# Sums of squares of eight norms: two products of 12-bit parts with ones in the place of one fp32 product

## Chip, cores and metric

The kernel runs on one core of a Trainium2 chip. The metric is the device time of one execution in microseconds; for the kernel before it is the median of three timed runs. One further execution was profiled; its trace is what the rows below come from.

## What is computed

Two transformer blocks follow each other on one sequence of 256 tokens with 1024 channels, each block with two layers, all in fp32. The first block has, per layer, a feed-forward, a hybrid mixer (a recurrent branch, an attention branch and a convolution branch) and a second feed-forward; the second block has a mixer and a feed-forward with a short convolution. Each of these parts begins with a norm:

```python
def rms_norm(x, g):
    xf = x.astype(jnp.float32)
    y = xf * lax.rsqrt(jnp.mean(xf * xf, axis=-1, keepdims=True) + NORM_EPS)
    return (y * g.astype(jnp.float32)).astype(x.dtype)

for l in range(DEPTH):
    x = x + 0.5 * swiglu(rms_norm(x, ffn1_norm[l]), ffn1_w1[l], ffn1_w2[l])
    x = x + hybrid_mixer(rms_norm(x, mix_norm[l]), positions, w_in[l], ...)
    x = x + 0.5 * swiglu(rms_norm(x, ffn2_norm[l]), ffn2_w1[l], ffn2_w2[l])
```

The change concerns the mean of squares in it, which is one number for each token, summed over 1024 channels.

## The kernel before

Activations lie with channels on the partitions: x is a tile of 128 partitions x 8 groups x 256 tokens, so a sum over channels is one over 8 groups (elementwise adds) and one over 128 partitions. A weight slab of 1024 columns is loaded by a DMA that SyncE issues (raw), rounded to 12-bit mantissas by ScalarE (wh, line 206) and its remainder taken by VectorE (wl, line 206 too). Activations are split the same way (xh and xl; hh and hl for the hidden units, function split, lines 511 to 513). Each product of fp32 matrices is then three products of such parts (mm3, lines 235 to 237): wh with xh, wh with xl, wl with xh. A slab feeds 24 of them, each with 128 x 128 weights and 256 columns. Six buffers each of wh and wl let ScalarE and VectorE work ahead of TensorE; four of raw let the transfers work ahead of them.

The norm is spread out. While x is written, Next.take splits x times the gain at once, without the root, and class Stat collects the squares: ScalarE squares each group (line 481, tile sq), VectorE adds them up (line 489, tile sqa). Stat.done (line 494) sums over the partitions: a product of a 128 x 128 tile of ones with the last sqa, in fp32, gives every partition the whole sum in a PSUM tile o. ScalarE makes the factor R of it in two activations (rstd_from, lines 466 and 467: logarithm and exponential). The products of the first weights run meanwhile on the values without the factor, and VectorE applies R to their sums when it reads them out of PSUM (line 620 in the first block's feed-forwards, line 1298 in the second's; in the mixers line 541 makes normalised values of x). So the work around a norm does not stop for it: the sum of squares is called from inside the first loop over weights (function linears, argument between; first_pairs for feed-forwards).

Seven PSUM banks hold sums of the feed-forward products (four in mixers); a bank is free again when VectorE has read it.

What sets the order on each engine is a scheduler that places the instructions by its own estimates of when operands are there; within an engine the queue is then strictly in order. Dependencies added by hand (behind) and program order for table loads bind it in some places. Stat.done has two further forms: late (the norm behind a part of the second block, which adds a second fp32 product) and tok (the norm ahead of the second block's mixer, which also wants the sum with tokens on partitions).

At the start, ScalarE's queue issues the DMA of the first 128 rows of parameters (line 122), which TensorE transposes (line 129) ahead of x itself (line 378).

Of the kernel before, what the change touches and what calls it, by code (L numbers as in the profile page):

```python
# [8 lines left out]
F32R = mybir.dt.float32r  # L9
# [7 lines left out]
P = 128  # L17
T = 256
# [25 lines left out]
def f32(ap):  # L44
    return ap.bitcast(F32)
# [95 lines left out]
def kernel(ctx: ExitStack, tc: tile.TileContext, p, out: bass.AP):  # L141
    nc = tc.nc
    V, S, G, PE = nc.vector, nc.scalar, nc.gpsimd, nc.tensor

    const = ctx.enter_context(tc.tile_pool(name="const", bufs=1))
    wpools = [ctx.enter_context(tc.tile_pool(name="w", bufs=6))]
    act = ctx.enter_context(tc.tile_pool(name="act", bufs=1))
# [136 lines left out]
    def linps():  # L284
        return banks['lin'].tile([P, 512], F32, name="lin")
# [2 lines left out]
    ident = const.tile([P, P], F32, name="ident")  # L288
    ones = const.tile([P, P], F32, name="ones")
    G.memset(ones, 1.0)  # L290
    G.affine_select(out=ident, in_=ones, pattern=[[-1, P]], compare_op=ALU.is_equal, fill=0.0, base=0,
                    channel_multiplier=1)
    epsc = const.tile([P, 1], F32, name="epsc")
# [22 lines left out]
    start = ctx.enter_context(ExitStack())  # L316
# [58 lines left out]
    for k in range(KD):  # L375
        ps = linps()
# [85 lines left out]
    def rstd_from(dst, ps, n, eps=epsc):  # L462

        t = tmp.tile([P, T], F32, name="sq")
        w = dst.shape[-1]
        S.activation(t[:, :w], ps, AF.Ln, scale=1.0 / n, bias=eps)
        S.activation(dst, t[:, :w], AF.Exp, scale=-0.5)
# [5 lines left out]
    class Stat:  # L473
# [17 lines left out]

        def done(self, tok=False):
            ps = pso.tile([P, 512], F32, name="o")
            PE.matmul(ps[:, :T], ones, self.acc, start=True, stop=not self.late)
            if self.late:
                PE.matmul(ps[:, :T], ones, self.sq, start=False, stop=True)
            r = act.tile([P, T], F32, name="R", bufs=2)
            rstd_from(r, ps[:, :T], D)
            if not tok:
                return r  # L500
            ps = banks['att'].tile([P, 512], F32, name="pt")
            for t in range(2):
                PE.matmul(ps[:, t:t + 1], self.acc[:, t * P:(t + 1) * P], ones[:, 0:1], start=True, stop=True)
            rt = act.tile([P, 2], F32, name="Rt", bufs=2)
            rstd_from(rt, ps[:, 0:2], D)
            return r, rt

    def split(h, lo, src, scale=None):

        if scale is None:  # L510
            return S.copy(h, src), V.tensor_tensor(lo, src, f32(h), op=ALU.subtract)
        return (S.activation(h, src, AF.Copy if isinstance(scale, float) else AF.Identity, scale=scale),
                V.scalar_tensor_tensor(lo, src, scale, f32(h), op0=ALU.mult, op1=ALU.subtract))
# [920 lines left out]
```

## Time and profile before

| | us |
|---|---|
| median of three timed runs | 1889.68 |
| lowest and highest of them | 1886.5, 1891.59 |
| the profiled execution | 1880.21 |
| its span, from first to last instruction | 1878.5 |

| engine | busy, us | share of the span |
|---|---|---|
| TensorE, products | 1850.9 | 99% |
| TensorE, weight loads | 1809.4 | 96% |
| VectorE | 1491.8 | 79% |
| ScalarE | 1121.2 | 60% |
| GpSimd | 75.8 | 4% |

How to read it: a product's row shows the time from its start to the modelled end, 0.28 us for an ordinary one, while products start every 0.11 us; so the cost of a product on TensorE is read from the starts of its neighbours. An fp32 product appears as two records. A share that is an average over the span says little about single places: VectorE's 79% has stretches of 100%.

### The profile page before, as it was taken

What the parts mean: (1) busy time and instruction counts of PE and PEld (TensorE: products, weight loads), DVE (VectorE), ACT (ScalarE), POOL (GpSimd) and SP (SyncE); (2) the same over time, 40 slices, a digit from 0 to 9 for tenths busy, and PEclk for the clock granted to TensorE, in tenths of its full rate; (3) what the DMA queues carried; (4) which work ended last, traced back from release to release, by engine and by line L of the source; (5) the groups of instructions that cost most, each with busy time, mean ns of one, the idle gap of its engine ahead of it and who ended that gap; (6) DMA issues with size and microseconds to landing.
All of it is one profiled execution on the core that took longest, in us unless ns stands there. A gap on an engine that the chain in (4) does not pass through costs nothing.

```text
span 1878.5 us, 38913 instructions
## 1 busy us (share of the span) xinstructions
PE 1850.9 (99%) x15292; PEld 1809.4 (96%) x15292; DVE 1491.8 (79%) x3041; ACT 1121.2 (60%) x1895; POOL 75.8 (4%) x225
## 2 busy tenths in 40 slices
PE   8999999999999999999999999999999999999998
PEld 8999999999999999999999999989999998999997
DVE  7778799897766776799987766888799778779983
ACT  6545777575555555668566555466666545757663
POOL 8000000000000000000000000110000011000000
PEclk9999999999999999999999999999999999999999
DMA  8656545556656665653546666561366647135652
GB/s 260 205 176 197 176 142 158 183 168 202 193 189 200 192 195 182 189 179 127 169 157 214 191 193 190 152 213 46 113 210 199 207 127 235 53 123 173 209 199 82
DMA packets 329879, 327.36 MB, mean 174 GB/s; under 512 B 16956, under 2 KB 323648, under 8 KB 329696
## 3 DMA queue, kind: packets, MB, share of 16 engines
q1 hardware_dynamic: 326336, 322.71, 55.2%
q0 software_dynamic: 3344, 2.16, 0.5%
q8 instruction: 120, 1.97, 0.4%
q14 instruction: 63, 0.52, 0.1%
q10 hardware_dynamic: 16, 0.00, 0.0%
HBM read 323.76 MB, written 1.05 MB: 173 GB/s over the span
## 4 chain that ended last, share of the span: by engine, by line
PE 93%; ACT 2%; DVE 2%; DMA 2%; issue 1%; SPq 0%; DVEq 0%; ACTq 0%
PE lin L235 27%; PE lin L236 27%; PE lin L237 27%; PE o L673 2%; PE lin L278 2%; PE lin L280 1%; PE lin L279 1%; PE sc L668 1%; PE pt L659 1%; DMA raw<-in_w_in_dram 1%; ACT wh L206 1%; DVE wl L206 1%; PE sc L667 1%; PE o L674 1%; DMA raw<-in_ffn_w_dram 0%
## 5 line engine op out<-in xcount | busy, mean ns | idle before, releaser
L206 DVE TENSOR_TENSOR wl<-raw,wh 128x1024 fp32r<-128x1024 f32 (+2 forms) x644 | 748.5, 1168 | 267.9 <-ACT wh L206 267.1
L206 ACT CAST wh<-raw 128x1024 fp32r<-128x1024 f32 (+2 forms) x644 | 644.6, 1005 | 473.7 <-PE lin L236 321.1
L235 PE MATMUL lin<-xh,wh 128*128 128x256 f32 (+1 forms) x3120 | 866.1, 279 | 3.8 <-ACT wh L206 2.3
L236 PE MATMUL lin<-xl,wh 128*128 128x256 f32 (+1 forms) x3120 | 869.4, 279 | 0.0
L237 PE MATMUL lin<-xh,wl 128*128 128x256 f32 (+1 forms) x3120 | 868.2, 279 | 0.0
L235 PEld LDWEIGHTS lin<-xh,wh 128*128 128x128 f32 (+1 forms) x3120 | 584.6, 188 | 6.7 <-ACT wh L206 2.9
L236 PEld LDWEIGHTS lin<-xl,wh 128*128 128x128 f32 (+1 forms) x3120 | 588.0, 189 | 0.7
L237 PEld LDWEIGHTS lin<-xh,wl 128*128 128x128 f32 (+1 forms) x3120 | 586.1, 188 | 0.5
L235 PE MATMUL lin<-hh,wh 128*128 128x256 f32 x880 | 243.0, 276 | 0.0
L236 PE MATMUL lin<-hl,wh 128*128 128x256 f32 x880 | 242.9, 276 | 0.0
L237 PE MATMUL lin<-hh,wl 128*128 128x256 f32 x880 | 242.9, 276 | 0.0
L235 PEld LDWEIGHTS lin<-hh,wh 128*128 128x128 f32 x880 | 165.2, 188 | 0.0
L236 PEld LDWEIGHTS lin<-hl,wh 128*128 128x128 f32 x880 | 165.2, 188 | 0.0
L237 PEld LDWEIGHTS lin<-hh,wl 128*128 128x128 f32 x880 | 165.2, 188 | 0.0
L235 PE MATMUL lin<-r,wh 128*128 128x256 f32 x372 | 105.6, 284 | 0.8 <-ACT f L898 0.5
L237 PE MATMUL lin<-r,wl 128*128 128x256 f32 x372 | 104.9, 282 | 0.0
L932 DVE SCALAR_TENSOR_TENSOR f<-f,pcol,f 128x256 f32<-128x256 f32 x240 | 103.9, 482 | 0.9
L236 PE MATMUL lin<-r,wh 128*128 128x256 f32 x372 | 103.9, 279 | 0.0
L622 ACT ACTIVATE sg<-g 128x256 f32<-128x256 f32 x88 | 35.6, 413 | 61.1 <-DVE g L620 61.0
L235 PEld LDWEIGHTS lin<-r,wh 128*128 128x128 f32 x372 | 70.1, 188 | 1.9 <-ACT f L898 0.9
L236 PEld LDWEIGHTS lin<-r,wh 128*128 128x128 f32 x372 | 70.0, 188 | 0.4
L237 PEld LDWEIGHTS lin<-r,wl 128*128 128x128 f32 x372 | 69.9, 188 | 0.2
(435 smaller groups left out, 2348.7 us busy)
## 6 DMA issues: line engine op xcount, KB each, us to landing
raw<-in_ffn_w_dram SPq DMA_DIRECT2D x256, 512.0 KB, 3.7
raw<-in_w_in_dram SPq DMA_DIRECT2D x116, 512.0 KB, 3.6
raw<-in_w_up_dram SPq DMA_DIRECT2D x88, 512.0 KB, 3.7
raw<-in_w_down_dram SPq DMA_DIRECT2D x42, 512.0 KB, 3.4
raw<-in_w_out_dram SPq DMA_DIRECT2D x32, 512.0 KB, 3.7
raw<-in_w_in_dram SPq DMA_DIRECT2D x32, 256.0 KB, 3.5
raw<-in_ffn_w_dram SPq DMA_DIRECT2D x16, 256.0 KB, 3.1
raw<-in_lru_w_out_dram SPq DMA_DIRECT2D x8, 512.0 KB, 4.7
```

The costliest lines, as they stand in the source:

```text
L206: i = S.copy(dst(h), src(raw)), V.tensor_tensor(dst(lo), src(raw), f32(dst(h)), op=ALU.subtract)
L235: PE.matmul(ps, wh, xh, start=first, stop=False)
L236: PE.matmul(ps, wh, xl, start=False, stop=False)
L237: PE.matmul(ps, wl, xh, start=False, stop=last)
L278: PE.matmul(ps, xh, wh, start=first and k == 0, stop=False)
L279: PE.matmul(ps, xh, wl, start=False, stop=False)
L280: PE.matmul(ps, xl, wh, start=False, stop=last and k == kt - 1)
L622: S.activation(sg_, g, AF.Silu)
L659: PE.transpose(pt[:, i * P:(i + 1) * P], e[:, i * P:(i + 1) * P], ident)
L667: PE.matmul(sc[:, 0:P], q[:, 0:P], k[:, 0:P], start=True, stop=True)
L673: PE.matmul(o[:, 0:T], v[:, 0, :], pt[:, 0:T], start=first, stop=False)
L932: i = V.scalar_tensor_tensor(cc[:, c, :], pcin[:, c, j:j + T], prm('cdw', l, 4 * j + c), cc[:, c, :], op0=ALU.mult, op1=ALU.add)
```

## The change

A second tile of ones, onesr, of the type fp32r (the one of the split parts), is made once at the start by ScalarE; it is a stretch of a tile twice as wide, so that later tiles keep their place within a kilobyte. In Stat.done the forms late and tok stay as they were. In the plain form, which eight norms use (the two feed-forwards and the mixer of both layers of the first block, and the feed-forwards of the second block), sqa is split into sah (ScalarE) and sal (VectorE), and two products with onesr add up both parts in the same PSUM tile.

```diff
+    onesr = const.tile([P, 2 * P], F32R, name="onesr")[:, 48:48 + P]
+    S.copy(onesr, ones)
...
-            PE.matmul(ps[:, :T], ones, self.acc, start=True, stop=not self.late)
-            if self.late:
-                PE.matmul(ps[:, :T], ones, self.sq, start=False, stop=True)
+            if self.late or tok:
+                PE.matmul(ps[:, :T], ones, self.acc, start=True, stop=not self.late)
+                if self.late:
+                    PE.matmul(ps[:, :T], ones, self.sq, start=False, stop=True)
+            else:
+
+                ah, al = (act.tile([P, T], F32R, name="sa" + q) for q in "hl")
+                split(ah, al, self.acc)
+                PE.matmul(ps[:, :T], onesr, ah, start=True, stop=False)
+                PE.matmul(ps[:, :T], onesr, al, start=False, stop=True)
```

The new instructions also make the scheduler order others anew. Line numbers of the new kernel are higher by 3 from line 291 on and by 10 behind Stat.done.

ScalarE at the norm of the first feed-forward. Line 481 (484) squares, line 206 converts a weight slab, lines 466 and 467 (469 and 470) make R, line 622 (632) begins the feed-forward's activations. Before:

```order
L481 ACTIVATE sq<-x 128x256
L206 CAST wh<-raw 128x1024 x2
L466 ACTIVATE sq<-o,epsc 128x256
L467 ACTIVATE R<-sq 128x256
L206 CAST wh<-raw 128x1024
L622 ACT_TABLE_LOAD
```

The same place now:

```order
L484 ACTIVATE sq<-x 128x256
L206 CAST wh<-raw 128x1024
L521 CAST sah<-sqa 128x256
L206 CAST wh<-raw 128x1024
L469 ACTIVATE sq<-o,epsc 128x256
L206 CAST wh<-raw 128x1024
L470 ACTIVATE R<-sq 128x256
L206 CAST wh<-raw 128x1024
L632 ACT_TABLE_LOAD
```

The new copy stands behind one conversion of weights, and a further conversion has come between the two activations that make R.

TensorE at the norm of the first block's mixer in layer 0 (o is the PSUM tile of the sum of squares, lin one of the weight products). Before:

```order
L235 MATMUL lin<-xh,wh 128x256
L236 MATMUL lin<-xl,wh 128x256
L237 MATMUL lin<-xh,wl 128x256
L494 MATMUL o<-sqa,ones 128x256
L235 MATMUL lin<-xh,wh 128x256
```

The same place now:

```order
L237 MATMUL lin<-xh,wl 128x256
L505 MATMUL o<-sah,onesr 128x256
L235 MATMUL lin<-xh,wh 128x256
L236 MATMUL lin<-xl,wh 128x256
L506 MATMUL o<-sal,onesr 128x256
```

The first product stands where the old one stood, the second two products later. In the first feed-forward the first stands three products later than the old one and the second eight behind it; in the second block's feed-forwards four later and six behind; in the other three feed-forwards both stand at the old place.

VectorE at the norm of the second block's first feed-forward (line 1298, now 1308, reads the sums out of PSUM with R). Before:

```order
L489 TENSOR_TENSOR sqa<-sqa,sq 128x256
L206 TENSOR_TENSOR wl<-raw,wh 128x1024 x2
L1298 TENSOR_TENSOR up_17796<-lin,R 128x256
L1298 TENSOR_TENSOR up_17797<-lin,R 128x256
L1298 TENSOR_TENSOR up_17798<-lin,R 128x256
L1302 SCALAR_TENSOR_TENSOR u<-up_17796,pcol_1980,u 128x256
```

The same place now:

```order
L492 TENSOR_TENSOR sqa<-sqa,sq 128x256
L206 TENSOR_TENSOR wl<-raw,wh 128x1024
L521 TENSOR_TENSOR sal<-sqa,sah 128x256
L206 TENSOR_TENSOR wl<-raw,wh 128x1024 x2
L1308 TENSOR_TENSOR up_17828<-lin,R 128x256
L1308 TENSOR_TENSOR up_17829<-lin,R 128x256
```

The subtraction stands between two conversions of weights, and a third conversion has moved ahead of the first reading; the fourth one, too, stands earlier than before among the operations of line 1312 (1302). From there the order on VectorE and ScalarE differs for the next hundred microseconds.

## Rows read from the trace of the kernel before

**Rows 1.** The page: busy time (share) and count; the chain that ended last.

```profile
PE 1850.9 (99%) x15292; PEld 1809.4 (96%) x15292; DVE 1491.8 (79%) x3041; ACT 1121.2 (60%) x1895; POOL 75.8 (4%) x225
...
PE 93%; ACT 2%; DVE 2%; DMA 2%; issue 1%; SPq 0%; DVEq 0%; ACTq 0%
```

**Rows 2.** Timeline, TensorE, third site: start, length, operation, idle before.

```profile
426.63 0.28 PE L236 MATMUL lin<-xl,wh 128*128 128x256 f32 x1
...
427.20 0.59 PE L494 MATMUL o<-sqa,ones 128*128 128x256 f32 x2
...
427.75 0.28 PE L236 MATMUL lin<-xl,wh 128*128 128x256 f32 x1
```

**Rows 3.** Groups by line, 0 to 60 us: count, busy us, mean ns, idle.

```profile
L511 DVE TENSOR_TENSOR hl<-u,hh 128x256 fp32r<-128x256 f32 x8 | 3.0, 418 | 0.0
L511 ACT CAST hh<-u 128x256 fp32r<-128x256 f32 x8 | 2.9, 402 | 0.9 <-DVE u L625 0.9
```

**Rows 4.** Timeline, VectorE and ScalarE, ahead of the third site.

```profile
421.48 0.42 DVE L489 TENSOR_TENSOR sqa<-sqa,sq 128x256 f32<-128x256 f32 x1
...
421.84 1.05 ACT L206 CAST wh<-raw 128x1024 fp32r<-128x1024 f32 x1 [0.95 <-PE lin L236]
```

**Rows 5.** Timeline, VectorE, ScalarE and TensorE, first site.

```profile
24.69 0.42 DVE L489 TENSOR_TENSOR sqa<-sqa,sq 128x256 f32<-128x256 f32 x1
...
25.41 1.05 ACT L206 CAST wh<-raw 128x1024 fp32r<-128x1024 f32 x1 [1.59 <-DMA raw<-in_ffn_w_dram]
...
25.53 0.59 PE L494 MATMUL o<-sqa,ones 128*128 128x256 f32 x2
...
26.49 1.23 DVE L206 TENSOR_TENSOR wl<-raw,wh 128x1024 fp32r<-128x1024 f32 x1 [1.39 <-ACT wh L206]
```

**Rows 6.** Timeline, VectorE and TensorE, second site (mixer, layer 0).

```profile
197.37 0.42 DVE L489 TENSOR_TENSOR sqa<-sqa,sq 128x256 f32<-128x256 f32 x1
197.71 0.82 DVE L206 TENSOR_TENSOR wl<-raw,wh 128x640 fp32r<-128x640 f32 x1
...
197.77 0.28 PE L237 MATMUL lin<-xh,wl 128*128 128x256 f32 x1
197.88 0.66 PE L494 MATMUL o<-sqa,ones 128*128 128x256 f32 x2
...
198.50 0.28 PE L236 MATMUL lin<-xl,wh 128*128 128x256 f32 x1
```

**Rows 7.** Timeline, ScalarE, VectorE and TensorE, seventh site (second block, layer 0).

```profile
1350.36 1.04 ACT L206 CAST wh<-raw 128x1024 fp32r<-128x1024 f32 x1
...
1351.05 2.35 DVE L206 TENSOR_TENSOR wl<-raw,wh 128x1024 fp32r<-128x1024 f32 x2
1353.32 1.07 DVE L1298 TENSOR_TENSOR up<-lin,R 128x256 f32<-128x256 f32 x3
...
1362.30 1.22 DVE L206 TENSOR_TENSOR wl<-raw,wh 128x1024 fp32r<-128x1024 f32 x1
...
1351.43 0.59 PE L494 MATMUL o<-sqa,ones 128*128 128x256 f32 x2
```

**Rows 8.** Timeline, ScalarE and TensorE, the start.

```profile
1.85 1.28 ACT L471 ACT_TABLE_LOAD   x1 [1.85 <-POOL ident L291]
...
8.99 1.04 ACT L206 CAST wh<-raw 128x1024 fp32r<-128x1024 f32 x1 [1.35 <-DMA raw<-in_ffn_w_dram]
...
3.48 0.45 PE L129 MATMUL lin<-ident,prow 128*128 128x128 f32 x1 [3.48 <-POOL crow L336]
...
5.06 3.46 PE L378 MATMUL lin<-ident,xin 128*128 128x128 f32 x15 [0.91 <-DMA xin<-in_x_dram]
```

**Rows 9.** Windows: stretch, length, busy (count) by engine, granted clock, DMA share.

```profile
12.50:16.20 3.70, 3.70 (x21) 3.70 (x20) 3.70 (x8) 3.20 (x6) 3.13 (x7) 0.54 0.94 272
...
1360.00:1380.00 20.00, 20.00 (x179) 20.00 (x179) 19.94 (x39) 13.15 (x22) 0.00 (x0) 1.00 0.63 195
```

**Rows 10.** Timeline, TensorE, the first weight product.

```profile
10.09 0.38 PE L235 MATMUL lin<-xh,wh 128*128 128x256 f32 x1 [1.57 <-ACT wh L206]
```

## Prediction

> **What bounds the kernel now.** I read the page first. TensorE is busy in 99% of the span, and the chain that ended last runs 93% over it [rows 1]: what a stage is worth on the other engines counts only where TensorE then waits. So the question for each of the eight changed norms is a small one: how many steps does TensorE's queue spend on the sum of squares, and does it stand still for the operands? For that I read the timelines of TensorE, ScalarE and VectorE around each place. The eight, in order of time, are: first block, layer 0, feed-forward 1 (25.53 us) [rows 5], mixer (197.88) [rows 6], feed-forward 2 (427.20) [rows 2]; layer 1 the same three; then the feed-forward of the second block's two layers (the first at 1351.43) [rows 7]. I call them sites 1 to 8.
>
> **Part 1: the product itself.** At site 3 nothing waits. Five products lie between 426.63 and 427.20, so an ordinary step is 0.57/5 = 0.114 us. From the fp32 product's start at 427.20 to the second product behind it at 427.75 pass 0.55 us; with one ordinary step taken off, the fp32 product costs 0.44 us of TensorE's queue [rows 2]. Its place is taken by two products of the kind that the whole kernel consists of (fp32r weights, 256 fp32r columns): 2 x 0.114 = 0.23. Saved: 0.21 us a site, 1.7 us for eight, if neither new product waits.
>
> **Part 2: the split.** ScalarE gets a copy that rounds to 12 bits (sah), VectorE a subtraction (sal). The same pair exists for the hidden units: 0.40 us and 0.42 us [rows 3]. Both engines have idle time, so the 8 x 0.4 us are no cost in themselves. What costs is that sah must follow the last sum sqa, sal must follow sah, each in its engine's queue behind a weight conversion, and TensorE takes its queue in order.
>
> *Sites 3, 4 and 6.* sqa is ready 5 us before TensorE gets there (last sum 421.48 to 421.90, product at 427.20), and ScalarE idles 0.95 us ahead of its next conversion [rows 2, 4]. Both parts are ready long before. Full gain: 3 x -0.21 = -0.6.
>
> *Site 1.* Here sah stands behind a weight conversion that itself waited 1.59 us for its transfer and ran 25.41 to 26.46; sqa was ready at 25.11 [rows 5]. So sah ends at about 26.8, and with the 0.09 us that pass between an end and the waiting product (197.79 to 197.88) [rows 6] TensorE may start it at 26.9. In the new order it comes three products later than the old one, at 25.53 + 3 x 0.114 = 25.87: a stand of 1.0 us. Eight products on, at 26.9 + 9 x 0.114 = 27.9, comes sal, which VectorE can begin only after its own conversion (26.49 to 27.72) [rows 5], so it ends at 28.1: another 0.2. Net: 1.2 + 0.23 - 0.44 = +1.0 us. TensorE never gets that back, since it has no idle time behind it to eat.
>
> R then is later by more than 1 us, also because a third conversion now stands between the two activations that make it. TensorE needs the first accumulator back only at product 156 of the stage, 44 products (5 us) behind the norm, and comes there later by 1.2 us itself. I count nothing, with 0.5 us as the upper bound.
>
> *Sites 2 and 5.* The old product already started at the moment that sqa came: end at 197.79, product at 197.88 [rows 6]. Now sah runs 197.88 to 198.28 and TensorE starts at 198.37 instead of 197.88: 0.49. Two products later (198.71) it wants sal, which follows VectorE's 640-column conversion (to 198.53) and ends at 198.87, so 198.96: 0.25. New cost 0.49 + 0.25 + 0.23 = 0.97; the old one is 198.50 - 197.77 less two steps = 0.50. Site 5 has the same order on all three engines. Net 2 x 0.47 = +0.9.
>
> *Sites 7 and 8.* sqa is complete when VectorE's next conversion starts, 1351.05; sah follows ScalarE's conversion that ends at 1351.40, so it is there at 1351.8. The new order has moved the product four steps back, to 1351.43 + 0.45 = 1351.88: no wait. sal follows the conversion that starts at 1351.05 (two of them take 2.35 us, so one ends near 1352.2) and ends near 1352.6; it is wanted six products later, at 1352.67 [rows 7]. No wait, by a hair: 2 x -0.21 = -0.4.
>
> **Part 3: what R's delay does at sites 7 and 8.** sal moved back makes R about 1.0 us later, and a third conversion now stands ahead of VectorE's first read of the sums (1353.32 before). I get 1354.8. Behind it VectorE is full: 19.94 of 20 us between 1360 and 1380 [rows 7, 9]. What it owes TensorE is wl. In the old order the fourth wl behind the norm was written from 1362.30 to 1363.52, and its slab (24 products; 81 of the stage lie ahead of the norm) is entered at about 1364.5, its first wl product two steps later: 1.2 us of margin. The new order pulls the third and the fourth wl ahead by several operations, which gives this slab more, and leaves the delay to later slabs. So I take 0 here, with the whole delay of 1.5 us a site as the bound; that is the likeliest way to a real loss.
>
> **Part 4: the start.** onesr is made by ScalarE ahead of everything else in its queue, including the DMA that brings the first parameter rows; and this first copy carries a table load of its own. The row of a table load is 1.28 us, with the next instruction free to start at once [rows 8]. With it and a 0.4 us copy, the DMA of those parameters, whose place was just ahead of the old first table load at 1.85, goes out 1.3 to 1.7 us later, and the transposes of the parameters (3.48) with it; those of x ran mostly from 5.06, held by their own data. They shift by 0.1 to 0.6 us. The first products wait for the conversion at 8.99, and that waits for its transfer with 1.35 us of ScalarE idle ahead of it [rows 8], so the cover is thicker than the shift: I take +0.1.
>
> The Trainium skill, page "ScalarE: Activation LUTs", section "What ACT_TABLE_LOAD costs", says that a switch of set costs about 1.28 us of load and about 1.38 us of drain. The load agrees with the row; the drain does not show in it. By the page the DMA would be another 1.4 us late, the shift at most 2.0 us against 1.35 of cover, and the sum up to 0.7 us higher (an estimate from that page).
>
> **Sum.** +1.0 (site 1) + 0.9 (2, 5) - 0.6 (3, 4, 6) - 0.4 (7, 8) + 0.1 (start) = +1.0 us. Against the profiled execution (1880.2 us, span 1878.5) that is 1881.2. The three timed runs of before lie higher, at 1886.5 to 1891.6, median 1889.7; the change has nothing to do with that offset, so I forecast 1890.7 for the median after.
>
> **Rivals.**
> *The parts are always ready.* If the order is right about when sah and sal come, all eight sites gain: -1.7 us, 1888.0. For it speaks that five or six sites show room; against it the rows of sites 1, 2 and 5, where the operand was just in time or its engine stood waiting. It would need ScalarE's transfer at site 1 to come a microsecond sooner. Chance 0.15, and still within 0.3% (5.7 us, about what a measurement of this kernel can tell from no change).
> *The clock falls at site 1.* TensorE's granted clock was 0.54 between 12.50 and 16.20, mostly at 1.2 instead of 2.4 GHz, after it had waited 1.57 us at 10.09 and again shortly after [rows 9, 10]. That stretch held 21 products in 3.70 us, which at 0.114 take 2.4: 1.3 us lost. A stand of 1.0 + 0.2 is near enough that it can happen again: 1892.0. Chance 0.2; also within 0.3%.
> *Slower: VectorE runs out of wl at sites 7 and 8.* If the reordered half of these stages (both feed-forwards are ordered anew for some 100 us) leaves VectorE later than its margin, TensorE stands for the difference at each slab where it is, until the margin is back. It decides from 1.2 us of delay beyond what the moved conversions give back. With 3 us at each site: 1890.7 + 6 = 1897. For it: VectorE's 19.94 of 20 us; against it: two conversions are pulled forward, and no wait of the product of that stage shows before. Chance 0.1.
> *Not what it says:* if products with onesr cost as much as fp32 ones, each site pays 0.65 more: 5 us, 1896. Every other product with fp32r operands steps at 0.114, so 0.02.
> *Faster by over 0.3%:* nothing in the sum can give more than 1.7 us; only a side effect that I don't see (all later tiles lie 1 or 3 KB further on in each partition), or the runs' own spread: 0.05.
>
> **How the numbers follow.** The forecast's own case has 0.48; with the first two rivals 0.83 lies within 0.3%. Slower by over 0.3% takes the third and fourth rival: 0.12. The range: the low end is the first rival less half the spread of the runs (2.5 us): 1885.5; the high end reaches to the slower rival's time: 1896.5.
>
> **What would show it.** In the profile after, TensorE's list of waits has the sah product for about 1 us once and 0.5 us twice, and the sal product for 0.2 to 0.3 three times, nowhere else; the step of both is 0.114; the sites at 427, 607 and 1011 show no wait and lie 0.2 closer to their neighbours. Waits for wl inside the last two feed-forwards would prove the slower rival; a clock below 1 near 27 us the second. I would be wrong if TensorE stands at sites 7 or 8, or if ordinary steps change from 0.114.

## The result, and the profile after

The change made the kernel slower by 1%, where I had forecast +1.0 us.

| | before | after |
|---|---|---|
| median of six runs each, us | 1885.7 | 1901.56 |
| lowest, highest | 1873.45, 1891.59 | 1897.98, 1908.75 |
| ratio after to before | | 1.0099, interval 1.0071 to 1.0128 |
| profiled execution, span | 1878.5 | 1899.8 |

With the later series before was timed 117 times in all (medians of the series 1879 to 1886, lowest run 1873.1, highest 1906.4) and after 18 times (median 1901.1, 1878.0 to 1913.3). That single runs of one kernel lie 30 us apart is part of the finding. In the second series of after the ratio reads 1.0031, because comparisons leave out runs over 1.5% above the fastest, which here drops runs that are long for the reason told below; the medians give 1899.38/1886.13 = 1.0070.

The page of after, busy times with counts and the chain that ended last [rows 1 before]:

```profile
PE 1869.7 (98%) x15292; PEld 1826.1 (96%) x15292; DVE 1497.9 (79%) x3049; ACT 1125.3 (59%) x1905; POOL 75.5 (4%) x225
...
PE 84%; DVE 10%; ACT 2%; DMA 2%; issue 1%; SPq 0%; DVEq 0%; ACTq 0%
```

As many products as before (one fp32 product was two records, so is a pair), 18.8 us longer busy. TensorE hardly waits more: the rows of its list of waits add up to 23.4 us against 20.9. It is the products themselves. Windows with nothing but ordinary products, of before and then of after (stretch, length, busy (count), granted clock, DMA share, GB/s):

```profile
60.00:120.00 60.00, 60.00 (x532) 1.00 0.62 194
450.00:600.00 150.00, 150.00 (x1326) 1.00 0.61 193
1040.00:1190.00 150.00, 150.00 (x1326) 1.00 0.62 191
1740.00:1800.00 60.00, 60.00 (x512) 1.00 0.63 203
```

```profile
60.00:120.00 60.00, 60.00 (x512) 1.00 0.60 186
450.00:600.00 150.00, 150.00 (x1276) 1.00 0.59 184
1040.00:1190.00 150.00, 150.00 (x1276) 1.00 0.59 183
1740.00:1800.00 60.00, 60.00 (x532) 1.00 0.71 218
```

The granted clock is 1.00 (the upper of its two levels, 2.4 GHz) in all eight, and TensorE is never idle in them. Still 150 us hold 1326 products or 1276: **the ordinary step has two values**, 113.3 ns (three products in 340) and 117.8 ns (three in 353.3). Each holds for some 10 to 430 us on end. Before has both too, in other stretches: its last window is long, that of after short. Weight loads tell the two apart; the stretch from 450 to 600 us, first before (short step), then after (long step; count, busy us, mean ns):

```profile
L235 PEld LDWEIGHTS lin<-xh,wh 128*128 128x128 f32 x266 | 49.9, 188 | 0.0
L237 PEld LDWEIGHTS lin<-xh,wl 128*128 128x128 f32 x266 | 49.9, 188 | 0.0
L236 PEld LDWEIGHTS lin<-xl,wh 128*128 128x128 f32 x265 | 49.7, 188 | 0.0
```

```profile
L235 PEld LDWEIGHTS lin<-xh,wh 128*128 128x128 f32 x274 | 52.6, 192 | 0.0
L237 PEld LDWEIGHTS lin<-xh,wl 128*128 128x128 f32 x275 | 51.6, 188 | 0.0
L236 PEld LDWEIGHTS lin<-xl,wh 128*128 128x128 f32 x274 | 51.4, 188 | 0.0
```

In the long step every third load takes 192 ns in the place of 188. Which of the three lines has it is constant within a stretch and differs between stretches; I call it the phase.

Over the whole trace (some 13,240 steps between neighbouring products of lines 235 to 237) the mean step was 114.62 ns before and 115.85 after. Measured from 113.33, that is 17.0 us and 33.3 us of long-step time: 16.3 of the 21.3 us between the two spans. Another 2.5 are the waits above. The remaining 2.5 I did not attribute.

The changed places themselves. TensorE at the third site [rows 2 before], where 0.35 us hold three steps and the pair costs what two ordinary products cost:

```profile
430.71 0.28 PE L237 MATMUL lin<-xh,wl 128*128 128x256 f32 x1
430.83 0.28 PE L505 MATMUL o<-sah,onesr 128*128 128x256 f32 x1
430.95 0.28 PE L506 MATMUL o<-sal,onesr 128*128 128x256 f32 x1
431.06 0.28 PE L235 MATMUL lin<-xh,wh 128*128 128x256 f32 x1
```

The first site, ScalarE and TensorE [rows 5]:

```profile
25.89 1.05 ACT L206 CAST wh<-raw 128x1024 fp32r<-128x1024 f32 x1 [1.53 <-DMA raw<-in_ffn_w_dram]
...
26.84 0.40 ACT L521 CAST sah<-sqa 128x256 fp32r<-128x256 f32 x1
...
27.35 0.33 PE L505 MATMUL o<-sah,onesr 128*128 128x256 f32 x1
...
28.31 0.28 PE L237 MATMUL lin<-xh,wl 128*128 128x256 f32 x1
28.58 0.38 PE L506 MATMUL o<-sal,onesr 128*128 128x256 f32 x1
```

The second site [rows 6]:

```profile
203.06 0.42 DVE L492 TENSOR_TENSOR sqa<-sqa,sq 128x256 f32<-128x256 f32 x1
...
203.51 0.41 ACT L521 CAST sah<-sqa 128x256 fp32r<-128x256 f32 x1 [0.72 <-DVE sqa L492]
203.54 0.28 PE L237 MATMUL lin<-xh,wl 128*128 128x256 f32 x1
...
203.97 0.39 PE L505 MATMUL o<-sah,onesr 128*128 128x256 f32 x1 [0.16 <-ACT sah L521]
...
204.60 0.39 PE L506 MATMUL o<-sal,onesr 128*128 128x256 f32 x1
```

And the start, ScalarE, its queue and TensorE [rows 8, 10]:

```profile
0.81 1.28 ACT L293 ACT_TABLE_LOAD   x1 [0.81 <-PEq L1432]
1.25 0.58 ACTq L122 DMA_DIRECT2D prow<-in_ffn_norm_dram  x1
2.10 0.30 ACT L293 CAST onesr<-ones 128x128 fp32r<-128x128 f32 x1
...
9.31 1.04 ACT L206 CAST wh<-raw 128x1024 fp32r<-128x1024 f32 x1 [1.74 <-DMA raw<-in_ffn_w_dram]
...
10.41 0.58 PE L235 MATMUL lin<-xh,wh 128*128 128x256 f32 x1 [0.89 <-ACT wh L206]
```

### The profile page after: what moved, and what is told of

Same layout as the page of the kernel before. It is cut to its first block, busy times and chain, and to the rows that moved or that the text cites. A ratio compares the mean times of both kernels' runs of the same rounds, so it can differ in the third digit from the quotient of the medians.

```text
span 1899.8 us, 38924 instructions
## 1 busy us (share of the span) xinstructions
PE 1869.7 (98%) x15292; PEld 1826.1 (96%) x15292; DVE 1497.9 (79%) x3049; ACT 1125.3 (59%) x1905; POOL 75.5 (4%) x225
## 4 chain that ended last, share of the span: by engine, by line
PE 84%; DVE 10%; ACT 2%; DMA 2%; issue 1%; SPq 0%; DVEq 0%; ACTq 0%
PE lin L235 24%; PE lin L237 24%; PE lin L236 24%; DVE wl L206 3%; DVE f L942 2%; PE o L683 2%; PE lin L278 1%; PE lin L280 1%; PE lin L279 1%; DMA raw<-in_w_in_dram 1%; PE sc L678 1%; PE pt L669 1%; ACT wh L206 1%; PE sc L677 1%; PE o L684 1%
```

## The experiments

All runs first, in groups. "Long" is the share of long steps in the run's one profile (mean step less 113.33, over 4.45), "excess" what they cost in us, "rest" the span less that. In p3 the column is a mean cost and no share: there three products took not only 340 ns (1,138 of 4,382 triples) or about 353, but also 360 (594) and 347 or 348 (628). The ratio is to runs of before on the same chip.

| kernel | median, us | ratio, interval | long | excess | span | rest |
|---|---|---|---|---|---|---|
| before (first profile) | | | 29% | 17.0 | 1878.5 | 1861.5 |
| e1_before_again | 1887.80 | 0.9966 to 1.0027 | 52% | 30.7 | 1897.3 | 1866.6 |
| e3_tiles_only | 1890.02 | 0.9976 to 1.0034 | 40% | 23.6 | 1886.8 | 1863.2 |
| e4_ones_copy | 1881.14 | 0.9945 to 1.0005 | 29% | 17.3 | 1884.1 | 1866.8 |
| c1_mixers | 1884.59 | 1.0013 to 1.0047 | 37% | 21.6 | 1890.8 | 1869.2 |
| f1_spare_ahead | 1883.16 | 0.9974 to 1.0027 | 17% | 10.0 | 1876.3 | 1866.3 |
| after (first profile) | 1901.56 | 1.0071 to 1.0128 | 57% | 33.3 | 1899.8 | 1866.5 |
| e2_after_again | 1899.38 | 0.9997 to 1.0064 | 47% | 27.7 | 1889.1 | 1861.4 |
| c2_ffns | 1902.60 | 1.0103 to 1.0142 | 43% | 25.1 | 1894.7 | 1869.6 |
| f3_sites346 | 1904.83 | 1.0080 to 1.0139 | 72% | 42.5 | 1905.8 | 1863.3 |
| f2_spare_behind | 1906.36 | 1.0096 to 1.0153 | 69% | 40.6 | 1905.3 | 1864.7 |
| p1_pad | 1872.36 | 0.9917 to 0.9959 | 8% | 4.6 | 1872.6 | 1868.0 |
| p2_pad_after | 1872.54 | 0.9917 to 0.9957 | 8% | 4.7 | 1870.8 | 1866.1 |
| p5_wl128 | 1872.31 | 0.9914 to 0.9969 | 4% | 2.5 | 1871.3 | 1868.8 |
| h1_off128 | 1882.89 | 0.9983 to 1.0023 | 12% | 6.9 | 1876.9 | 1870.0 |
| p4_pad256 | 1883.17 | 0.9966 to 1.0010 | 14% | 8.1 | 1878.4 | 1870.3 |
| s256_shift | 1884.29 | 0.9988 to 1.0038 | 29% | 16.8 | 1882.6 | 1865.8 |
| s128_shift | 1923.59 | 1.0184 to 1.0233 | 93% | 54.7 | 1923.3 | 1868.6 |
| s384_shift | 1921.99 | 1.0206 to 1.0246 | 97% | 57.1 | 1921.2 | 1864.1 |
| p3_pad64 | 1910.80 | 1.0119 to 1.0179 | 79% | 46.8 | 1908.0 | 1861.2 |

Over twenty profiles the spans go from 1871 to 1923 us, the rests only from 1861 to 1870: the long step is what sets these kernels apart. Two profiles of one kernel can lie 14 us apart in it (17.0 and 30.7 for before), so which kernel is slower is read from the medians of the runs.

### Is the step a matter of the program, its addresses, or the execution?

Both kernels once more, without an edit.

> The kernel before once more, unchanged, to see whether the step between ordinary products (113.3 ns in some stretches, 117.8 ns in others; 28% of the steps at the longer one in the first profile of before) is a property of the program or of the execution. Theory A (addresses) and theory B (order and timing of the stream): the stretches repeat, share 25 to 31%, span 1877 to 1881 us. Theory C (each execution draws anew): the stretches lie elsewhere, share anywhere between 10 and 60%, span between 1868 and 1898. Ratio to before 1.000 for all three, with an interval that shows how wide the draws are.

> The changed kernel once more, unchanged. Theories A and B: the same stretches as in its first profile (long step from 12 to 141 us, 376 to 809 and 973 to 1232; share 56%), span 1897 to 1903, ratio 1.007 to 1.013. Theory C: other stretches and another share, and a ratio that may fall to 1.000.

The stretches didn't repeat: before, at 52%, had the long step from 400 to 806 us, where its first profile was short from 381 to 798. So the execution draws part of it (theory C). But after stayed above before in its medians.

Then before with the new tiles alone, and with the copy of ones alone:

```diff
+    onesr = const.tile([P, 2 * P], F32R, name="onesr")[:, 48:48 + P]
+    S.copy(onesr, ones)          # e4 only
...
+            if not (self.late or tok):          # e3 only
+                ah, al = (act.tile([P, T], F32R, name="sa" + q) for q in "hl")
```

> The kernel before with the three new tiles allocated and never used: every instruction and its order as before, every tile at its address in the changed kernel (1024 bytes further from the constants on, 3072 bytes from R on). Theory A (the addresses choose the step): share of long steps as in the changed kernel, 50 to 60%, 1899 to 1904 us, ratio 1.008 to 1.012. Theory B (interruptions of the product stream choose): as before, share 25 to 31%, ratio 0.998 to 1.002. Theory C: any share, with other stretches than either.

> The kernel before with only the second tile of ones made at the start (a copy on ScalarE with a table load of its own; the tile moves all others by 1024 bytes); nothing uses it, all eight norms are the fp32 product of before. The start is some 1.3 us later on ScalarE. Theory A: 1024 bytes may or may not do what 3072 do; a share like that of the run with the tiles alone would speak for it. Theory B: the first stage, 12 to 141 us, takes the long step, as in the changed kernel (130 us of 4%: +5 us), and the stages behind it may go either way; ratio 1.002 to 1.006 if they stay as before. Theory C: no relation.

Neither is slower. Tiles 1 or 3 KB further on don't matter (theory A falls in this form), nor does the copy at the start; the 1.002 to 1.006 that theory B gave for e4 didn't come. In e4 the first stage began in the long step, as in after, but it ended at 28 us, right behind the fp32 product of site 1 (27.4). In after it went on to 141 us.

### Which of the norms bring the loss?

The change at the mixers' two norms alone, and at the six feed-forwards' alone (the other norms keep the fp32 product):

```diff
-            if self.late or tok:
+            if self.late or tok or mix != True:      # c1; False in c2
```

> The change at the two mixers' norms alone (sites 2 and 5), the six feed-forward norms as before; the tile of ones is made at the start as in the changed kernel. Theory M (a pair at a feed-forward norm leaves the long step as it is, in 5 of 5 cases without a wait, where an fp32 product ended it in 2 of 4; so the loss comes from the feed-forward norms): like before, 1883 to 1889 us, ratio 0.998 to 1.002, share of long steps 25 to 45%. Rival N (the waits for sah and sal at the mixers' norms, 0.28 to 0.43 us each, set the step of the mixer and of all that follows): 1895 to 1902, ratio 1.005 to 1.009, share 45 to 60%. The forecast's own cost for these two sites, +0.9 us, is in both.

> The change at the six feed-forward norms alone, the two mixers' norms as before. Theory M: like the changed kernel, 1895 to 1902 us, ratio 1.005 to 1.009, share 45 to 60%. Rival N: 1883 to 1889, share 25 to 45%. If the loss is split, both kernels lie at 1890 to 1893.

The feed-forwards bring it: 1.0122 against 1.0030. Both lie above their ranges of theory M (1.005 to 1.009 and 0.998 to 1.002), and why c1 is 0.3% slower I can't say. Their windows show how. First c1, then c2, ahead of and behind site 3:

```profile
405.00:425.00 20.00, 20.00 (x173) 1.00 0.66 212
440.00:600.00 160.00, 160.00 (x1414) 1.00 0.64 194
```

```profile
405.00:425.00 20.00, 20.00 (x172) 1.00 0.65 201
440.00:600.00 160.00, 160.00 (x1361) 1.00 0.60 185
```

Both come to the norm in the long step, with the long load on line 237. In c1 the fp32 product ends it; its row, and the neighbours:

```profile
432.17 0.28 PE L237 MATMUL lin<-xh,wl 128*128 128x256 f32 x1
432.28 0.59 PE L498 MATMUL o<-sqa,ones 128*128 128x256 f32 x2
432.53 0.47 PE L235 MATMUL lin<-xh,wh 128*128 128x256 f32 x1
432.83 0.28 PE L236 MATMUL lin<-xl,wh 128*128 128x256 f32 x1
```

An fp32 product steps otherwise (118, 216, 28 and 306 ns between starts) and so interrupts the rhythm. In c2 the pair steps like any two products, the rhythm goes on, and with nothing to interrupt it the long step holds to 795 us: some 3,100 products by 4.45 ns, 14 us from one place.

All cases at sites 1, 3, 4 and 6 that were met in the long step and where no wait mixes in, over the 14 traces with weight tiles at 64 modulo 256 bytes (320 or 64 modulo 512, below):

| met in the long step by | goes on long | ends |
|---|---|---|
| fp32 product right behind the product with the long load | 0 | 6 (c1, e3, f1, p4 twice; e4 at site 1) |
| fp32 product elsewhere in the three | 7 (e1 twice, c1, h1, f2 three times) | 0 |
| pair alone | 10 (after 3, e2 2, c2 2, f3 3) | 0 |

Left out for its waits is site 1 in after, f1 and f3; in f3 the fp32 product stood elsewhere in the three, waited 0.2 us for sqa, and the long step ended a few products behind it. Met in the short step and without a wait, the stream stayed short behind fp32 product and pair alike (for the pair two cases, site 6 in e2 and c2). Behind a pair the long load has moved from line 237 to line 235: it recurs every third product, whatever the operands are.

One difference was not tested by itself. The tile ones, which the fp32 product loads as weights, lies at 128 modulo 512 bytes in every one of these kernels; onesr lies at 320, where wh and wl are in before and after. No kernel moved either of them, so the table doesn't tell whether the fp32 product ends the long step by its own steps or by the place of its weights.

### Is it the missing fp32 product?

The change at sites 3, 4 and 6 alone; then the changed kernel with a spare fp32 product ahead of, or behind, each feed-forward pair:

```diff
-            if self.late or tok:
+            if self.late or tok or fence['site'] not in (3, 4, 6):      # f3
...
+                if not mix:                                              # f1, f2
+                    PE.matmul(ps[:, T:], ones, self.acc, start=True, stop=True)
                 PE.matmul(ps[:, :T], onesr, ah, start=True, stop=False)
                 PE.matmul(ps[:, :T], onesr, al, start=False, stop=True)  # f2: spare behind it
```

> The change at sites 3, 4 and 6 alone (both inner feed-forwards and the last of the first block), where nothing waits; apart from the three pairs and the tile of ones every engine's order is that of before. The forecast's own sum for these is -0.6 us. Theory M (a missing fp32 product leaves the long step on): 1.006 to 1.013 of before if the stream comes to site 3 in a long step, as it did in most traces of kernels with the changed start; the long step then holds over sites 3 and 4, from 376 or 400 to 800 us. Rival (the loss comes from sites 1, 7 and 8, where both engines are ordered anew): 0.998 to 1.003, and a long step that comes to site 3 ends there or at site 4.

> The changed kernel with a spare fp32 product of the old kind (ones and the last sum, into a part of the sum's PSUM tile that nobody reads) just ahead of each feed-forward pair: 6 x 0.44 = 2.6 us of work more. Theory M: at sites 3, 4 and 6 a long step ends if the product ahead of the spare one has the long load; ratio to before 0.999 to 1.005 although work was added to the kernel that was 0.8% slower. Rival (the pairs or their order cost): 1.009 to 1.014, the changed kernel's plus 2.6 us.

> The same with the spare fp32 product behind each pair, two products later, so that it meets another of the three phases. Theory M with the rule of the phase: a stretch that comes to site 3 with its long load on the product of line 237 (four of seven such arrivals so far) is not ended here, one on another line is; ratio 1.004 to 1.013. If any fp32 product does: 0.999 to 1.005. Rival (pairs cost): 1.009 to 1.014.

Three changed norms without any wait bring the whole loss (1.0109); the tile of ones that comes with them cost nothing by itself (e4). Work added ahead of the pairs takes it away (1.000), and the same work two products later doesn't (1.0125). Windows of f1 and then f2, ahead of and behind site 6; both arrive long, with line 237 in phase, and only f1 leaves short:

```profile
985.00:1005.00 20.00, 20.00 (x172) 1.00 0.67 209
1040.00:1190.00 150.00, 150.00 (x1326) 1.00 0.63 190
```

```profile
985.00:1005.00 20.00, 20.00 (x172) 1.00 0.37 119
1040.00:1190.00 150.00, 150.00 (x1276) 1.00 0.59 183
```

One thing here is not settled: f1 came to site 3 short already, f2 and f3 long. What puts the stream into the long step ahead of the site is decided at interruptions of other kinds. At the first wait of that stage and of the same stage in layer 1 (400 and 984 us in before) a step of 221 to 223 ns left the stream short in all seven cases of the first six traces, one of 226 or 227 left it long in both; in the other three the stream was long already and no such wait came. That is a matter of nanoseconds, and I can't say why some kernels mostly arrive long.

### What ends the long step: the place of the weights

In nine of nine cases of the first six traces the long step ended in the mixers' slab of 160 columns, whose rows lie 640 bytes apart. So I moved the weights. Before, all tiles wh and wl lie at 320 modulo 512 bytes. p1 and p2 make them 128 bytes longer (four places in turn), in before and in the changed kernel; the s kernels move all of them together; h1 adds three products with weights 128 bytes off at some twenty places; p3 and p4 lengthen by 64 and 256 bytes; p5 moves wl alone. Fillers behind are shortened so that the other tiles keep their places modulo 512. Apart from h1, all instructions and their order stay as they were.

```diff
-            h = wpool.tile([P, SL], F32R, name="wh")...
-            lo = wpool.tile([P, SL], F32R, name="wl")...
+            h = wpool.tile([P, SL + 32], F32R, name="wh")...     # p1, p2; + 16 in p3, + 64 in p4
+            lo = wpool.tile([P, SL + 32], F32R, name="wl")...
...
+    wpools[0].tile([P, 32], F32, name="gapw", bufs=1)      # s128, ahead of all weights; 64 in s256, 96 in s384
...
+            gap(wpool, 128, "gapl")                               # p5, once, ahead of the first wl
...
+                    if fence.pop('mend', 0):                      # h1
+                        for w_, x_ in ((s.h, a.h), (s.h, a.l), (s.l, a.h)):
+                            PE.matmul(ps[:, :T], w_[:, 0, 32:160], x_[:, k0, :], start=True, stop=True)
```

> The kernel before with each of its weight tiles wh and wl 128 bytes longer (4224 in the place of 4096), so that the tiles lie at different places modulo 512 bytes (320, 448, 64 and 192 in turn) where before all lay at 320. Same instructions in the same order. In nine of nine cases the long step ended within four products of the slab of 160 columns in the mixers (behind 206.9 us in the first profile of before), whose rows lie 640 bytes apart, so that its loads come from other places modulo 512. Theory A (a change of the place that weights are loaded from ends the long step): with another place every 24 products the share of long steps falls below 10%, 1863 to 1872 us, ratio 0.986 to 0.992. Theory B (only interruptions of the stream matter, that slab healed by its 96-column products or by chance): share 25 to 55% as in the six profiles so far, ratio 0.996 to 1.004. Rival C: other places than 320 are slower for themselves, ratio above 1.004.

> The changed kernel with the same longer weight tiles. If the long step is gone in both (theory A), the pair of these two runs shows what the changed norms themselves cost: the forecast's +1.0 us, 0.9995 to 1.0015 of the other, and the 1% of the first comparison is gone. If the change has a cost of its own in the size first measured (rival: 16 to 21 us), this kernel stays 1% above the other. Theory B: share 45 to 60%, 1893 to 1903 us.

> The kernel before with all weight tiles 128 bytes further, uniformly: 448 modulo 512 in the place of 320; moving operands where they were; same instructions and order. Tells a mere place from a change of place. If it is the alternation that ends the long step (theory A): share 25 to 55% as before, ratio 0.996 to 1.004. If the place 320 itself is what allows the long step: share below 10%, ratio 0.986 to 0.992. If 448 is worse in itself: ordinary steps longer than 113.3 ns everywhere and a ratio above 1.004.

> The kernel before with three extra products at 20 places (third pair of columns of each feed-forward's first half, three places in each first-block mixer, three in each second-block mixer), whose weights are columns 32 to 159 of the slab that comes next, so 128 bytes off; the product behind them overwrites their sums. They cost 60 x 0.113 = 6.8 us. Theory A: each place turns the long step into the short one (never the other way), share below 15%, 1868 to 1880 us, ratio 0.990 to 0.997 with their own cost in it. Theory B: share 25 to 55%, ratio 1.002 to 1.006. Some neighbouring instructions on VectorE and ScalarE are ordered otherwise than before (a few us either way).

p1 fell by 0.6% (0.9938, less than the forecast 0.986 to 0.992; the share, 8%, is within its range). Its six runs lie within 3.5 us of each other, where the 17 of before that were timed with it lie within 14.4, and all 117 within 33. p2, the changed kernel, is its equal: mean -0.2 us, with a standard error of 0.7. That pair prices the change itself. s128 took the third of its expectations: the long step nearly everywhere. The windows from 450 to 600 us of p1, p2 and s128:

```profile
450.00:600.00 150.00, 150.00 (x1325) 1.00 0.62 191
```

```profile
450.00:600.00 150.00, 150.00 (x1326) 1.00 0.61 191
```

```profile
450.00:600.00 150.00, 150.00 (x1276) 1.00 0.59 184
```

h1 missed its range (1.0003 for 0.990 to 0.997), though its one profile is 12% long. Two of its twenty places met a long stream of ordinary products (35.8 and 1539.0 us), and it ended there, in the second case with a wait of 0.09 us at the same place. Most others were met short or stood right behind products of another shape; from one of these (847.5 us) the stream ran long, so three products off the place don't always leave it short. Their own work, by the forecast 6.8 us, is in the time.

> The kernel before with all weight tiles 256 bytes further: 64 modulo 512. At 320 the share of long steps was 29 to 52% over executions, at 448 93%, in turn at 320, 448, 64 and 192 8%. If the place decides how firmly the long step holds, then 64 or 192 must be where it doesn't hold: share below 10% in at least one of the two, 1863 to 1872 us, ratio 0.986 to 0.993. If it is only the alternation that ends it (rival): share 25 to 95% at 64 and at 192 too, 1880 to 1925 us.

> The kernel before with all weight tiles 384 bytes further: 192 modulo 512. As for 64: place decides, share below 10% in at least one of the two, 1863 to 1872 us; only the alternation helps (rival), 25 to 95%, 1880 to 1925 us.

> The kernel before with each weight tile 64 bytes longer in the place of 128, so that the tiles lie at eight places modulo 512. If the change of place within 256 bytes is what ends the long step: as with 128 bytes, share below 10%, 1868 to 1876 us, ratio 0.991 to 0.997. If only the two classes (64 and 192 modulo 256) matter and the places between them are worse, 0.998 to 1.010; if smaller steps keep the stream short more firmly, below 0.991.

> The kernel before with each weight tile 256 bytes longer: they lie at 320 and 64 modulo 512 in turn, both 64 modulo 256. If it takes a change between the classes modulo 256 to end the long step: as before, share 25 to 55%, ratio 0.997 to 1.004. If any change of place does it (rival): share below 10%, ratio 0.991 to 0.996.

> The kernel before with the tiles wl alone 128 bytes further: wh at 320, wl at 448 modulo 512; the class changes twice in every three products. If each change between classes works against the long step: share below 10%, 0.987 to 0.995. If it is a change against the rhythm of three that breaks it, and a change with the rhythm holds it (rival): a share far off 30%, 60% or more, 1.008 to 1.022.

No single place is free of it, so of the two theories for s256 and s384 the alternation holds (97% for s384, a little above its 95). 320 and 64 behave alike, 448 and 192 alike: what counts is the place modulo 256. At 64 the step is left to chance, at 192 it is long. Turning between 320 and 64 (p4) left time and spread as they were (its one profile has 14%, in neither range); turning between the classes (p1, p2), or having wh in one and wl in the other (p5), makes the short step the one that holds. With places in between as well (p3, eight places in turn) the kernel is slower than with one place at 64 modulo 256: 1.0149, above the 1.010 that I had allowed. At 192 modulo 256 the long step comes without the long load; of s128, 450 to 600 us:

```profile
L236 PEld LDWEIGHTS lin<-xl,wh 128*128 128x128 f32 x291 | 54.7, 188 | 0.0
L237 PEld LDWEIGHTS lin<-xh,wl 128*128 128x128 f32 x291 | 54.6, 188 | 0.0
L235 PEld LDWEIGHTS lin<-xh,wh 128*128 128x128 f32 x290 | 54.2, 187 | 0.0
```

So the load of 192 ns goes with the long step at 64 modulo 256 and is not its cause everywhere.

p5 needs 128 bytes in a partition and is as fast as p1: both beat the kernel before by 0.6% and the changed one by more.

## Why the prediction was wrong

*The place itself: right.* Beyond ordinary steps of 113.3 ns, counted from the product ahead of a site to the thirtieth behind it (0.13 us taken off where these are long), the fp32 product cost 0.46 us at sites 3, 4 and 6 (forecast 0.44), the pair 0.23 (forecast 0.23), and nothing waited there.

*Sites 2 and 5: right.* Old 0.49 and 0.71, new 0.97 and 1.12: +0.48 and +0.41, forecast +0.47 each. The wait for sah shows above: from 203.54 to 203.97 less one step, 0.32 us.

*Site 1: right in kind, the size a draw.* Forecast: sah wanted at 25.87 and there at 26.9, a stand of 1.0 and a net +1.0. In the profile of after TensorE was itself later and hardly stood (27.35; 0.16 at sal): +0.1. In e2 and p2 the place cost 0.9 and 0.8 more than in before and p1. But the old product can stand there too: in e1 it cost 1.15, against 0.46 in the first profile of before.

*Sites 7 and 8: right.* -0.15 and -0.1, forecast -0.2 each. Part 3 was right too: R's delay cost TensorE no wait for wl.

*Part 4, the start: nothing.* The first product came at 10.41 in the place of 10.09 (forecast +0.1), but that is a draw: it came between 9.73 and 10.69 in the 11 profiles without the copy (mean 10.22) and between 9.87 and 10.53 in the 9 with it (mean 10.18). The DMA of the parameters was not late at all: 1.25, and 1.24 before, since the new table load began early, at 0.81, and the issue went out while it ran. The drain of the Trainium skill's page "ScalarE: Activation LUTs", section "What ACT_TABLE_LOAD costs", doesn't show here either: load to 2.09, copy at 2.10.

*The sum* of the eight places in the first two profiles is about 0, and p2 against p1 gives -0.2 with an error of 0.7; forecast +1.0. Nearly the whole difference is site 1. The pair doesn't rule the forecast out: 1.2 us is less than two of its errors.

**The step that failed** is the one under all of it: "an ordinary step is 0.57/5 = 0.114 us", taken once at site 3 and used for the whole kernel, with the remark that I would be wrong "if ordinary steps change from 0.114". They do, and did already before. The windows 60 to 120 (x532) and 1740 to 1800 us (x512) of before had it on show, 4% apart with the same work, clock and no wait. I looked at one window of that kind [rows 9] and at no second.

The second error follows: the runs lay 6 to 11 us above the profiled execution, and I wrote that "the change has nothing to do with that offset". Those were three runs; the next three lay between 1873.5 and 1884.9. By the later profiles the offset was the long step's draw, and the change acts on just that. So the fp32 product, which I priced as pure cost, had a side use: in one phase of three it puts a long stream right for the next 200 to 400 us. Taking it out saved 0.23 us where nothing waits and lost up to 14.

*The rivals.* "Always ready", the clock, VectorE and the price of onesr: none of them. The granted clock was 1.00 from 26 to 30 us, where site 1 lies, and in every window shown; the two products at site 3 step like ordinary ones; no wait for wl shows at sites 7 and 8. That "all later tiles lie 1 or 3 KB further on", which I named as a chance for a gain, was tried (e3) and does nothing; moving the tiles wl alone by 128 bytes gives 0.6% (p5). My range ended at 1896.5 and left out what made both the spread of the runs and the loss.

## What to carry to other kernels

Before costing an edit by an "ordinary step", count the products in several windows of every stage: where counts differ by some per cent at the same clock and without waits, the stream has more than one step, and an edit that adds or removes an interruption is priced by the stretch behind it, not by itself. Take such a lottery out first (here by laying the two kinds of weight tiles 128 bytes apart modulo 256); then small edits can be measured, and 0.6% came with it. When runs of one kernel differ by 1% and the profile shows no wait, look for it in the step.

## What the hardware showed that I had not expected

A stream of 128 x 128 fp32r weights with 256 columns each ran at 113.3 or 117.8 ns a product. It stayed there until something interrupted it or the place of its weights changed. The step by place of the weight tiles: 64 modulo 256 either value (14 to 72% long in one profile each, with every third load at 192 ns in the long step and 188 otherwise), 192 modulo 256 93 to 97% long (all loads at 187 or 188), both in turn 4 to 8%. With eight places 64 bytes apart further values came, such as 120 ns (three products in 360, p3). All this was with the moving operands at 0 modulo 256, which I did not move.

By the Trainium skill, page "TensorE: Matmul & The Clock Gate", section "Wait — 56ns, not 53.3ns?", products at the upper clock follow each other at their columns over 2.4 GHz plus about 2.5 ns, which is 109.2 ns for 256 (an estimate from that page). Neither step agrees; each product here also has a load of its own.

The same page, section "Step-by-step: what each phase is for", says that loading the next weights takes no read bandwidth from the running product. The runs show that where the weights lie changes the step by 4%; what inside the chip does that, no run here shows, and it stays open.
